# Named PSUM banks in two feed-forward layers, a later Silu and modulation stream, sums on VectorE, and a third ordinary pair in the last two

## The chip, the cores and the metric

The kernel runs as one program on one core of a Trainium2 chip. The core has five engines that work side by side, each through its own queue in order: TensorE (PE in the rows; its weight loads, PEld, overlap it), VectorE (DVE), ScalarE (ACT), GpSimd (POOL) and SyncE (SP), which issues the transfers. They wait for one another by semaphores. TensorE writes its results into PSUM, which has eight banks; one 128x512 tile of float32 fills a bank. The metric is the time of one execution on the device in microseconds (us).

## What is computed

A float32 tensor x of 512 tokens by 1024 channels goes through eight residual stages: an attention mixer and a feed-forward layer with modulation, twice, then a state-space mixer, a feed-forward layer, a convolution module and a feed-forward layer, and a last norm. The stages of the change are the four feed-forward layers. In the first block they read

```python
cond = jax.nn.silu(c)
mod = cond @ ada_w[l] + ada_b[l]
sh1, sc1, g1, sh2, sc2, g2 = [m[:, None, :] for m in jnp.split(mod, 6, axis=-1)]
...
h = _rms_norm(x, norm_ffn[l]) * (1.0 + sc2) + sh2
x = x + g2 * _swiglu(h, ffn_gate[l], ffn_up[l], ffn_down[l])
```

and in the second `h = h + swiglu_ffn(rmsnorm(h, ffn_norm[i]), w_gate, w_up, w_down)`, where swiglu is `(silu(h @ wg) * (h @ wu)) @ wd` with a hidden width of 2816, 22 chunks of 128.

## The kernel before

**Layout and products.** x is kept transposed, as eight chunks of 128 channels by 512 tokens (`xT`, `X[c]`). Every float32 product is three matmuls: each operand is split into a rounded part `hi` and a rest `lo`, and `mm3` (and the same lines in `lin`) issues hi·hi (L305), lo·hi (L306) and hi·lo (L307) into one accumulator. The split of a weight is one cast on ScalarE (L297) and one subtraction on VectorE (L298), each 1024 wide; weights come by a load on SP (L291, or L708 in `seven`), through three buffers.

**Stages.** They run in the order mix0, ffn0, mix1, ffn1, ssm, ffn2, conv, ffn3, final. Each has its own PSUM pool. Within a stage the code is written as items and woven streams, and a scheduler then sets each engine's order at build time.

**The norm ahead of a stage.** ffn0 and ffn1 use the class `Split`, which works on halves of 256 tokens: `stats` puts the sums of squares into a PSUM tile `ss` (L462) and takes the reciprocal root on VectorE (it begins with `rm`, L345); `spread` broadcasts it into a PSUM tile `rb` (L471); `build` makes, for each chunk, z = x·gain·rb on VectorE (L481), hi on ScalarE (L491, or L487 and L488), and lo on VectorE for even chunks (L492) and on GpSimd for odd ones (L489). `Split.lin` interleaves this with the first two hidden chunks: all matmuls of the first half, 256 wide, then those of the second. A half of the two pairs of accumulators `pg` and `pu` is 96 matmuls, six for a chunk and pair. ffn2 and ffn3 use the class `Norm`: the matmuls run on data without the scale, `rb` (L374) is copied to `R` on ScalarE (L427), and the scale is multiplied in behind the products (L794, L796).

**The modulation.** `cond` loads c into `cb` (L625) and applies Silu (L626). `Mod.stream` takes a column pair at a time: load `araw` (L641), multiply by `cb` and sum on VectorE (L651). In ffn0 a stream of 28 such pairs, 56 products, is woven into the layer, behind `nm.mark`, the last z.

**Pairs in a feed-forward layer.** For each of the 22 hidden chunks there is one pair of gate and up products. An ordinary pair has 48 matmuls of 128x512. From number FIRST_S[n] on, the pairs use `seven`, which replaces eight half products by seven, 84 matmuls of 128x256, and for that needs sums of quarters of the normed data. `sums` makes them with `crossed`, for k = 0 to 3 (chunks k and k + 4): two subtractions on GpSimd (L687, L688), two on VectorE (L689, L690), a cast `xh` on ScalarE (L692) and the rest `xl` on VectorE for even k and on GpSimd for odd k (L693). In ffn2 and ffn3 the z for it comes from ScalarE (L761). FIRST_S was (22, 3, 2, 2): ffn0 has ordinary pairs only, ffn1 three, ffn2 and ffn3 two.

**Banks.** The six accumulators, one tile for sums and one for broadcasts were given to the pool by counts (`"mm": 6, "st": 1, "tr": 1`), and the pool set the banks. In both ffn0 and ffn1 the first `pg` had bank 0, the first `pu` bank 5, and the next ones 4, 3, 2 and 1; `ss` had 6 and `rb` 7 in the layer. The tiles of the mixer ahead, the `rb` of the first half among them, have their banks from that mixer's pool: the bank of `rb` was 0 ahead of ffn0 and 5 ahead of ffn1.

## Time and profile before

| | us |
|---|---|
| median of three runs | 2677.18 |
| the runs | 2670.21, 2677.18, 2677.36 |
| profiled execution | 2673.64 |
| its span, first to last instruction | 2671.9 |
| time around the span | 1.7 |
| mean granted TensorE clock | 0.974 |

Where the profile speaks of idle time before an instruction, the bracket names what released it. ffn0 runs from about 369 to 739 us in it, ffn1 from 945 to 1310, ffn2 from 1725 to 2065 and ffn3 from 2310 to 2645.

### The profile page before, as it was taken

To read this page: it belongs to the slowest core of one execution; us is meant where nothing else is said; L and a number is where in the kernel's file an instruction comes from. 1 tells how busy PE (TensorE), PEld (TensorE's weight loads), DVE (VectorE), ACT (ScalarE), POOL (GpSimd) and SP (SyncE) were. 2 spreads that over 40 slices of the span, in tenths; PEclk is the share of its full clock that TensorE was granted. 3 is DMA by queue.
4 is the path that set the end of the run, shared out by engine and by line. 5 is a ranking of instruction groups with operands and counts; after the bars stand their busy time and mean duration, and the time that the engine had idled before them with its cause. 6 is when DMAs were issued, how large, how long until landed. Compare 5 with 4: busy or idle time off the path is not lost.

```text
span 2671.9 us, 39622 instructions
## 1 busy us (share of the span) xinstructions
PE 2529.7 (95%) x15167; PEld 2231.6 (84%) x15167; DVE 1943.4 (73%) x3437; ACT 1261.9 (47%) x2324; POOL 549.1 (21%) x394
## 2 busy tenths in 40 slices
PE   5887989999999989999999999999999998899998
PEld 3666888888888889999788888789999788799997
DVE  8898756555556686677678887678677797678776
ACT  4456642222357554544455444455445555545443
POOL 3344220000112250000100000131012683321102
PEclk9889999999999989999999999999999998999999
DMA  7711025555421113333322121223333110133332
GB/s 262 238 56 40 32 87 205 174 167 199 146 81 41 40 64 95 101 99 104 110 73 72 52 87 59 81 81 108 104 103 109 66 63 17 64 112 101 102 98 87
DMA packets 84734, 265.77 MB, mean 99 GB/s; under 512 B 9280, under 2 KB 11712, under 8 KB 84544
## 3 DMA queue, kind: packets, MB, share of 16 engines
q1 hardware_dynamic: 84544, 263.24, 30.4%
q8 instruction: 119, 1.95, 0.3%
q14 instruction: 71, 0.58, 0.1%
HBM read 261.10 MB, written 2.10 MB: 99 GB/s over the span
## 4 chain that ended last, share of the span: by engine, by line
PE 72%; DVE 14%; ACT 4%; issue 3%; POOL 3%; DMA 3%; SPq 0%; DVEq 0%; POOLq 0%; ACTq 0%
PE pj L305 10%; PE pj L306 9%; PE pj L307 9%; PE pg L305 6%; PE pg L307 6%; PE pg L306 5%; PE pu L305 4%; PE pu L306 4%; PE pu L307 4%; DVE lo L298 2%; DMA raw<-w_gu 1%; POOL yp L1609 1%; DMA araw<-ada 1%; PE pj L1412 1%; PE pj L1413 1%
## 5 line engine op out<-in xcount | busy, mean ns | idle before, releaser
L297 ACT CAST hi<-raw 128x1024 fp32r<-128x1024 f32 (+5 forms) x445 | 393.7, 893 | 691.7 <-PE pj L306 260.5
L298 DVE TENSOR_TENSOR lo<-raw,hi 128x1024 fp32r<-128x1024 f32 (+5 forms) x435 | 461.6, 1064 | 175.2 <-ACT hi L297 172.1
L305 PE MATMUL pj<-d,hi 128*128 128x512 f32 (+1 forms) x940 | 354.3, 385 | 3.3 <-DVE xT L679 1.7
L306 PE MATMUL pj<-d,hi 128*128 128x512 f32 (+1 forms) x940 | 354.6, 380 | 0.0
L307 PE MATMUL pj<-d,lo 128*128 128x512 f32 (+1 forms) x940 | 351.5, 380 | 0.0
L741 POOL TENSOR_TENSOR bu<-bu 128x256 f32<-128x256 f32 x59 | 110.0, 1864 | 770.6 <-ACT bu L737 754.5
L305 PE MATMUL pu<-hi 128*128 128x256 f32 (+1 forms) x736 | 230.2, 314 | 3.2 <-DVE z L481 3.2
L307 PE MATMUL pu<-hi,lo 128*128 128x256 f32 (+1 forms) x736 | 231.1, 314 | 0.2 <-DVE lo L298 0.2
L306 PE MATMUL pu<-lo,hi 128*128 128x256 f32 (+1 forms) x736 | 229.9, 313 | 0.0
L305 PE MATMUL pj<-hi 128*128 128x512 f32 (+2 forms) x520 | 207.7, 403 | 3.9 <-ACT qk L901 1.2
L306 PE MATMUL pj<-lo,hi 128*128 128x512 f32 (+2 forms) x520 | 207.1, 398 | 3.6 <-DVE lo L492 2.4
L305 PEld LDWEIGHTS pj<-d,hi 128*128 128x128 f32 x940 | 177.7, 190 | 38.0 <-DVE xT L679 2.3
L306 PEld LDWEIGHTS pj<-d,hi 128*128 128x128 f32 x940 | 178.3, 190 | 33.2 <-issue 1.0
L307 PEld LDWEIGHTS pj<-d,lo 128*128 128x128 f32 x940 | 177.9, 189 | 33.3 <-issue 0.5
L307 PE MATMUL pj<-hi,lo 128*128 128x512 f32 (+2 forms) x520 | 204.8, 395 | 0.3 <-DVE lo L298 0.3
L305 PE MATMUL pg<-xh,hi 128*128 128x256 f32 x708 | 199.3, 282 | 0.8 <-ACT ua L734 0.7
L305 PE MATMUL pg<-hi 128*128 128x256 f32 (+1 forms) x572 | 192.6, 337 | 6.9 <-DVE z L481 4.5
L307 PE MATMUL pg<-xh,lo 128*128 128x256 f32 x708 | 198.0, 280 | 0.0
L306 PE MATMUL pg<-xl,hi 128*128 128x256 f32 x708 | 198.0, 280 | 0.0
L307 PE MATMUL pg<-hi,lo 128*128 128x256 f32 (+1 forms) x572 | 192.4, 336 | 4.8 <-DVE lo L298 4.8
L306 PE MATMUL pg<-lo,hi 128*128 128x256 f32 (+1 forms) x572 | 191.6, 335 | 0.6 <-DVE lo L492 0.6
L297 ACT CAST hi<-ws 128x1024 fp32r<-128x1024 f32 x118 | 123.5, 1049 | 116.7 <-DVE ws L711 48.5
(485 smaller groups left out, 6390.7 us busy)
## 6 DMA issues: line engine op xcount, KB each, us to landing
raw<-w_gu SPq DMA_DIRECT2D x176, 512.0 KB, 3.8
araw<-ada SPq DMA_DIRECT2D x96, 512.0 KB, 5.9
raw<-w_dn SPq DMA_DIRECT2D x48, 384.0 KB, 3.2
raw<-w_dn SPq DMA_DIRECT2D x48, 320.0 KB, 3.0
raw<-w_p SPq DMA_DIRECT2D x24, 512.0 KB, 3.6
raw<-w_out SPq DMA_DIRECT2D x32, 256.0 KB, 2.8
raw<-w_xs SPq DMA_DIRECT2D x16, 512.0 KB, 3.4
raw<-w_z SPq DMA_DIRECT2D x16, 512.0 KB, 3.4
```

What stands on the lines that cost most here:

```text
L297: S.copy(hi, raw)
L298: (eng or V).tensor_tensor(lo, raw, hi.bitcast(F32), op=OP.subtract)
L305: E.matmul(ps, lh, rh, start=start, stop=False, **k)
L306: E.matmul(ps, lh, rl, start=False, stop=False, **k)
L307: E.matmul(ps, ll, rh, start=False, stop=stop, **k)
L741: G.tensor_tensor(bu[:, :hv], bu[:, :hv], bu[:, hv:], op=OP.add)
L1412: E.matmul(o, xh[:, ts], wh[:, k], start=st_, stop=False, skip_group_check=True)
L1413: E.matmul(o, xh[:, ts], wl[:, k], start=False, stop=False, skip_group_check=True)
L1609: G.tensor_tensor(yp[:, sft:], yp[:, sft:], pr[:, sft:], op=OP.add)
```

## The change

It has four parts. In ffn0 and ffn1 the PSUM banks are named; with the lists below, the first `pg` of ffn0 has bank 7 and the first `pu` 4, those of ffn1 7 and 6; `ss` and `rb` have 1 and 6, and 4 and 5. In ffn0 the Silu of `cb` becomes a step that is emitted after four others, and the modulation stream comes behind `nm.lmark`, the last lo of the norm, and has weight 30. In ffn1 the sums of `crossed` are all on VectorE, two k behind the first item and two behind the second. FIRST_S becomes (22, 3, 3, 3): in ffn2 and ffn3 the third pair is an ordinary one. Lines from 245 on stand some ten lines lower in the code of the change.

```diff
-FIRST_S = (22, 3, 2, 2)
+FIRST_S = (22, 3, 3, 3)
...
-    "ffn0": ({"araw": 6, "cb": 2, "d": 16, "z": 3, "su": 2, "sq": 2}, {"mm": 6, "st": 1, "tr": 1}),
-    "ffn1": ({"d": 12, "z": 8, "sq": 2, "ws": 3, "xh": 4, "xl": 4, "ua": 2, "bu": 2}, {"mm": 6, "st": 1, "tr": 1}),
+    "ffn0": ({"araw": 6, "cb": 2, "d": 16, "z": 3, "su": 2, "sq": 2},
+             {"mm": (7, 4, 2, 3, 0, 5), "st": (1,), "tr": (6,)}),
+    "ffn1": ({"d": 12, "z": 8, "sq": 2, "ws": 3, "xh": 4, "xl": 4, "ua": 2, "bu": 2},
+             {"mm": (7, 6, 0, 1, 2, 3), "st": (4,), "tr": (5,)}),
...
+            if k == "ps" and isinstance(PHASES[name][1]["mm" if name != "start" else "pi"], tuple):
+                turn.clear()
+                for b in range(8):
+                    p.tile([128, T], F32, tag=f"b{b}", name=f"b{b}", bufs=1)
...
+        if isinstance(bufs[tag], tuple):
+            i = turn[tag] = turn.get(tag, -1) + 1
+            return p.tile(shape, dt, tag=f"b{bufs[tag][i % len(bufs[tag])]}", name=name, bufs=1)
...
-                    V.scalar_tensor_tensor(lo, z, sh, hi_.bitcast(F32), op0=OP.add, op1=OP.subtract)
+                    self.lmark = V.scalar_tensor_tensor(lo, z, sh, hi_.bitcast(F32), op0=OP.add, op1=OP.subtract)
...
-        S.activation(cbx[0], cbx[0], AF.Silu)
+        return lambda: S.activation(cbx[0], cbx[0], AF.Silu)
...
-    def crossed(k, z1, z2, pool_lo):
+    def crossed(z1, z2, eng, lo_eng):
...
-        G.tensor_tensor(q[0], z1[:, :hv], z1[:, hv:], op=OP.subtract)
-        G.tensor_tensor(q[2], z2[:, hv:], z1[:, hv:], op=OP.subtract)
+        eng.tensor_tensor(q[0], z1[:, :hv], z1[:, hv:], op=OP.subtract)
+        eng.tensor_tensor(q[2], z2[:, hv:], z1[:, hv:], op=OP.subtract)
...
-        (G if pool_lo else V).tensor_tensor(lo, t, hi.bitcast(F32), op=OP.subtract)
+        lo_eng.tensor_tensor(lo, t, hi.bitcast(F32), op=OP.subtract)
...
-                x4.append(crossed(k, *z, k % 2))
+                x4.append(crossed(*z, V if direct else G, G if k % 2 and not direct else V))
...
-                    sums(range(4) if direct else range(2 * js[0], 2 * js[0] + 2))
+                    sums(range(len(x4), len(x4) + 2))
...
-                cond()
-                _weave((f, 345), (behind(lambda: nm.mark, chain(md0.stream(range(20, 24)), md1.stream(range(24)))), 28))
+                silu = cond()
+
+                def later():
+                    for _ in range(4):
+                        yield 0.5
+                    silu()
+                    yield 0.0
+
+                _weave((f, 345), (chain(later(), behind(lambda: nm.lmark, chain(md0.stream(range(20, 24)),
+                                                                               md1.stream(range(24))))), 30))
```

The scheduler makes of this new orders on the engines at the starts of the four layers, and in ffn0 for the modulation through the whole layer; mix0, mix1, the body of ssm and conv keep theirs. In the rows that follow, the numbers are those of the buffers, and lines of the changed kernel are its own.

VectorE in ffn0, from the last lo of the second half (`lo_3493`) to the first weight split of the third and fourth pair of operands (L298, `lo_3814` before and `lo_3809` after); first before, then with the change.

```order
L492 SCALAR_TENSOR_TENSOR lo_3493<-z_3680,mod0_95,hi_3492 128x256
L651 ISA araw_3808,mod0_95<-araw_3808,cb_3513,vec_71 128x1024
L651 ISA mod0_95 128x1
L651 ISA araw_3880,mod0_95<-araw_3880,cb_3513,vec_71 128x1024
L651 ISA mod0_95 128x1
L651 ISA araw_3883,mod0_95<-araw_3883,cb_3513,vec_71 128x1024
L651 ISA mod0_95 128x1
L298 TENSOR_TENSOR lo_3814<-raw_3811,hi_3813 128x1024
```

```order
L502 SCALAR_TENSOR_TENSOR lo_3493<-z_3687,mod0_95,hi_3492 128x256
L661 ISA araw_3876,mod0_95<-araw_3876,cb_3521,vec_71 128x1024
L661 ISA mod0_95 128x1
L661 ISA araw_3879,mod0_95<-araw_3879,cb_3521,vec_71 128x1024
L661 ISA mod0_95 128x1
L308 TENSOR_TENSOR lo_3809<-raw_3806,hi_3808 128x1024
```

Before, three products of the modulation stood ahead of that lo and three between it and the split; with the change two stand between them and none ahead. On ScalarE the Silu of `cb` has the same place in both orders, behind the first half's build and ahead of the second's, and on SP the load of `cb` stands behind two loads of `w_gu` in both, with six loads of `araw` behind it before and two with the change.

VectorE in ffn1, up to the weight split for the first ordinary-width matmuls (`lo_8978` before, `lo_8974` after).

```order
L492 SCALAR_TENSOR_TENSOR lo_8624<-z_8666,mod1_100,hi_8623 128x256
L689 SCALAR_TENSOR_TENSOR ws_8923<-z_8664,ws_8923 128x256
L690 SCALAR_TENSOR_TENSOR ws_8923<-ws_8923,z_8664 128x256
L689 SCALAR_TENSOR_TENSOR ws_8932<-z_8665,ws_8932 128x256
L690 SCALAR_TENSOR_TENSOR ws_8932<-ws_8932,z_8665 128x256
L689 SCALAR_TENSOR_TENSOR ws_8943<-z_8666,ws_8943 128x256
L690 SCALAR_TENSOR_TENSOR ws_8943<-ws_8943,z_8666 128x256
L693 TENSOR_TENSOR xl_8929<-ws_8923,xh_8928 128x1024
L693 TENSOR_TENSOR xl_8949<-ws_8943,xh_8948 128x1024
L298 TENSOR_TENSOR lo_8978<-raw_8975,hi_8977 128x1024
```

```order
L699 SCALAR_TENSOR_TENSOR ws_9035<-z_8682,ws_9035 128x256
L700 SCALAR_TENSOR_TENSOR ws_8939<-ws_8939,z_8680 128x256
L700 SCALAR_TENSOR_TENSOR ws_8948<-ws_8948,z_8681 128x256
L700 SCALAR_TENSOR_TENSOR ws_9035<-ws_9035,z_8682 128x256
L703 TENSOR_TENSOR xl_8945<-ws_8939,xh_8944 128x1024
L703 TENSOR_TENSOR xl_8954<-ws_8948,xh_8953 128x1024
L697 TENSOR_TENSOR ws_9044<-z_8679 128x256
L698 TENSOR_TENSOR ws_9044<-z_8683,z_8679 128x256
L703 TENSOR_TENSOR xl_9041<-ws_9035,xh_9040 128x1024
L699 SCALAR_TENSOR_TENSOR ws_9044<-z_8683,ws_9044 128x256
L308 TENSOR_TENSOR lo_8974<-raw_8971,hi_8973 128x1024
```

Before, six sums of three k and two `xl` stood ahead of the split on VectorE, and the subtractions L687 and L688 and the `xl` of odd k on GpSimd. With the change 15 operations of sums and three `xl` (L703) stand there, of which the last eleven rows are shown, and GpSimd has none.

TensorE in ffn2 behind the broadcast `rb`; `pg_16453` and `pu_16454` are the second ordinary pair before and `pg_16565` is the first `seven`; with the change `pu_16470` is of the second pair and `pg_16567` and `pu_16568` are the third. First before, at `rb`,

```order
L374 MATMUL rb_16424<-cst_73,rstd_16405 128x128 x4
L307 MATMUL pu_16454<-hi_16242,lo_16450 128x512
L305 MATMUL pg_16453<-hi_16269,hi_16443 128x512
L306 MATMUL pg_16453<-lo_16270,hi_16443 128x512
L307 MATMUL pg_16453<-hi_16269,lo_16444 128x512
L305 MATMUL pu_16454<-hi_16269,hi_16449 128x512
```

then before, on TensorE a few rows on, at the end of the second pair,

```order
L306 MATMUL pg_16453<-lo_16297,hi_16443 128x512
L307 MATMUL pg_16453<-hi_16296,lo_16444 128x512
L305 MATMUL pu_16454<-hi_16296,hi_16449 128x512
L306 MATMUL pu_16454<-lo_16297,hi_16449 128x512
L307 MATMUL pu_16454<-hi_16296,lo_16450 128x512
L305 MATMUL pg_16565<-hi_16108,hi_16545 128x256
```

and last with the change, from `rb` on.

```order
L384 MATMUL rb_16440<-cst_73,rstd_16421 128x128 x4
L315 MATMUL pu_16470<-hi_16312,hi_16465 128x512
L316 MATMUL pu_16470<-lo_16313,hi_16465 128x512
L317 MATMUL pu_16470<-hi_16312,lo_16466 128x512
L315 MATMUL pg_16567<-hi_16124,hi_16557 128x512
L316 MATMUL pg_16567<-lo_16125,hi_16557 128x512
L317 MATMUL pg_16567<-hi_16124,lo_16558 128x512
L315 MATMUL pu_16568<-hi_16124,hi_16563 128x512
```

Before, 13 matmuls of 512 stood between `rb` and the first `seven`; with the change `rb` is ten matmuls later, and 51 of 512 stand behind it. ffn3 has the same change. In all, 72 matmuls fewer are issued.

## Rows read from the trace of the kernel before

**Rows 1.** The page: busy time of each engine in us, share of the span and instructions, and the share of each engine in the chain of work that ended last.

```profile
PE 2529.7 (95%) x15167; PEld 2231.6 (84%) x15167; DVE 1943.4 (73%) x3437; ACT 1261.9 (47%) x2324; POOL 549.1 (21%) x394
...
PE 72%; DVE 14%; ACT 4%; issue 3%; POOL 3%; DMA 3%; SPq 0%; DVEq 0%; POOLq 0%; ACTq 0%
```

**Rows 2.** Windows, a stretch in the middle of ffn0: from and to, length, busy time (with the count of instructions) of PE, PEld, DVE, ACT and POOL, granted TensorE clock, mean share of the DMA engines, GB/s.

```profile
420.00:520.00 100.00, 100.00 (x441) 82.43 (x440) 53.55 (x75) 23.96 (x28) 0.00 (x0) 1.00 0.52 173
```

**Rows 3.** Timeline of PE at the start of ffn0: start in us, duration, engine, line, operation, out<-in, shape, count, and in brackets the idle time before it and what ended it.

```profile
367.00 0.53 PE L471 MATMUL rb<-cst,rstdh 128*128 128x128 f32 x2
...
373.41 0.36 PE L305 MATMUL pg<-hi 128*128 128x256 f32 x1 [4.47 <-DVE z L481]
...
374.24 0.42 PE L305 MATMUL pg<-hi 128*128 128x256 f32 x1
...
398.65 0.40 PE L305 MATMUL pg<-hi 128*128 128x512 f32 x1
...
401.87 0.80 PE L307 MATMUL pg<-hi,lo 128*128 128x512 f32 x1 [2.59 <-DVE lo L298]
...
404.95 0.40 PE L305 MATMUL pg<-hi 128*128 128x512 f32 x1
```

**Rows 4.** Timelines of PE, ACT and POOL from the end of the ssm stage to the first seven pair of ffn2, with the same columns.

```profile
1721.72 0.39 PE L305 MATMUL pu<-hi 128*128 128x512 f32 x1
...
1727.61 0.39 PE L307 MATMUL pu<-hi,lo 128*128 128x512 f32 x1
...
1737.62 0.60 PE L374 MATMUL rb<-cst,rstd 128*128 128x128 f32 x4
...
1741.03 0.28 PE L305 MATMUL pg<-hi 128*128 128x256 f32 x1
...
1743.78 0.28 PE L307 MATMUL pu<-hi,lo 128*128 128x256 f32 x1
1746.72 0.58 PE L305 MATMUL pu<-xh,hi 128*128 128x256 f32 x1 [2.66 <-ACT hi L297]
...
1749.46 0.58 PE L307 MATMUL pu<-xh,lo 128*128 128x256 f32 x1 [1.51 <-DVE lo L298]
...
1753.73 0.28 PE L307 MATMUL pu<-xh,lo 128*128 128x256 f32 x1
...
1745.62 1.04 ACT L297 CAST hi<-ws 128x1024 fp32r<-128x1024 f32 x1
...
1748.22 5.23 POOL L693 TENSOR_TENSOR xl<-ws,xh 128x1024 fp32r<-128x1024 f32 x1 [5.65 <-ACT xh L692]
```

**Rows 5.** Timeline of PE at the start of ffn1.

```profile
951.66 0.55 PE L305 MATMUL pu<-hi 128*128 128x256 f32 x1 [3.17 <-DVE z L481]
...
957.56 0.62 PE L462 MATMUL ss<-ones,acc 128*128 128x1 f32 x4
...
978.18 0.40 PE L305 MATMUL pg<-hi 128*128 128x512 f32 x1
...
980.57 0.50 PE L307 MATMUL pg<-hi,lo 128*128 128x512 f32 x1 [1.76 <-DVE lo L298]
...
984.92 0.49 PE L305 MATMUL pg<-hi 128*128 128x512 f32 x1
```

**Rows 6.** Timeline of PE at the first seven pair of ffn3.

```profile
2329.91 0.28 PE L307 MATMUL pu<-hi,lo 128*128 128x256 f32 x1
2332.85 0.39 PE L305 MATMUL pu<-xh,hi 128*128 128x256 f32 x1 [2.65 <-ACT hi L297]
...
2335.58 0.58 PE L307 MATMUL pu<-xh,lo 128*128 128x256 f32 x1 [1.92 <-DVE lo L298]
...
2340.22 0.28 PE L306 MATMUL pg<-xl,hi 128*128 128x256 f32 x1
```

**Rows 7.** Timelines of DVE and ACT at the start of ffn0.

```profile
376.68 0.47 DVE L492 SCALAR_TENSOR_TENSOR lo<-z,mod,hi 128x256 fp32r<-128x256 f32 x1
...
384.50 1.06 ACT L626 ACTIVATE cb<-cb 128x1024 f32<-128x1024 f32 x1 [8.96 <-DMA cb<-c]
...
398.13 1.28 DVE L651 CUSTOM_DVE_ANT_0 araw<-araw,cb,vec 128x1024 f32<-128x1024 f32 x1 [1.52 <-DMA araw<-ada]
...
400.60 1.22 DVE L298 TENSOR_TENSOR lo<-raw,hi 128x1024 fp32r<-128x1024 f32 x1
```

**Rows 8.** Timeline of DVE at the start of ffn1.

```profile
954.95 0.95 DVE L492 SCALAR_TENSOR_TENSOR lo<-z,mod,hi 128x256 fp32r<-128x256 f32 x1
...
958.23 0.16 DVE L345 TENSOR_SCALAR rm<-ss 128x2 f32<-128x2 f32 x1 [2.32 <-PE ss L462]
...
965.69 2.69 DVE L492 SCALAR_TENSOR_TENSOR lo<-z,mod,hi 128x256 fp32r<-128x256 f32 x4
969.01 0.94 DVE L689 SCALAR_TENSOR_TENSOR ws<-z,ws 128x256 f32<-128x256 f32 x1 [0.63 <-POOL ws L687]
...
974.28 4.57 DVE L693 TENSOR_TENSOR xl<-ws,xh 128x1024 fp32r<-128x1024 f32 x2
978.77 1.75 DVE L298 TENSOR_TENSOR lo<-raw,hi 128x1024 fp32r<-128x1024 f32 x1
...
981.04 0.41 DVE L689 SCALAR_TENSOR_TENSOR ws<-z,ws 128x256 f32<-128x256 f32 x1
```

**Rows 9.** Waits of DVE from 365 to 740 us, which is ffn0: what waited and for whom, us in total, times, longest.

```profile
DVE araw L651 <- DMA araw<-ada: 85.1, 28, 6.7
```

More of the change, by code (lines that the diff above doesn't have):

```diff
@@ L231, in _program @@
     cur = {"sb": None, "ps": None}
+    turn = {}
     def phase(name, kinds=("sb", "ps")):
@@ L491, in build @@
                     S.activation(hi_, z, AF.Identity, bias=sh)
-                    V.scalar_tensor_tensor(lo, z, sh, hi_.bitcast(F32), op0=OP.add, op1=OP.subtract)
+                    self.lmark = V.scalar_tensor_tensor(lo, z, sh, hi_.bitcast(F32), op0=OP.add, op1=OP.subtract)
                 else:
                     S.copy(hi_, z)
-                    V.tensor_tensor(lo, z, hi_.bitcast(F32), op=OP.subtract)
+                    self.lmark = V.tensor_tensor(lo, z, hi_.bitcast(F32), op=OP.subtract)
         def lin(self, sets, at=(5, 10)):
@@ L974, in mix0 @@
         phase("start", ("ps",))
-        cond()
+        cond()()
         consts()
@@ L1798, in _program @@
         if stages[0] in STAGES[:4]:
-            cond()
+            cond()()
             mods()
@@ L1821, in _program @@
             if n == 0:
-                cond()
-                _weave((f, 345), (behind(lambda: nm.mark, chain(md0.stream(range(20, 24)), md1.stream(range(24)))), 28))
+                silu = cond()
[6 more added lines that the diff above has]
+                                                                               md1.stream(range(24))))), 30))
             else:
```

## The prediction

> **What bounds the kernel now.** I read the busy shares first: TensorE (PE) is busy 95% of the span, and the chain that ended last lies to 72% on PE and to 14% on VectorE (DVE) [rows 1]. So time is to be had only where PE stands still or runs at the lower clock, and I looked for those places in PE's timeline. The body of the first feed-forward layer shows none: in 420 to 520 us PE is busy for 100.00 of 100 us at a granted clock of 1.00 [rows 2]. The gaps lie at the starts of the four feed-forward layers, where the norm's result has to be built, and these are the places that the change touches.
>
> In ffn0 PE sees the broadcast `rb` at 367.00 and issues the first gate matmul at 373.41, after 4.47 us idle that ended with a z (L481) on DVE [rows 3]. A matmul on one half cannot need all z of that half; it waits because its accumulator lies in the bank that holds `rb`, which every z reads. Then its 256-wide matmuls take 0.21 instead of 0.12 us for a while (from 374.24 on, the granted clock at the 1.2 GHz level after the idle time). At 401.87 a second gap ends: 2.59 us for one `lo` (L298) on DVE, and the seven 512-wide matmuls from there to 404.95 take 3.08 us, where seven at the usual 0.2265 us take 1.59 (26 starts between 1721.72 and 1727.61, 5.89 us) [rows 3, 4]. ffn1 has the same pair of gaps: 3.17 us at 951.66, here on `pu`, and 1.76 us at 980.57 [rows 5]. ffn2 and ffn3 have theirs at the first `seven` pair: 2.66 and 1.51 us, and 2.65 and 1.92 us [rows 4, 6].
>
> **ffn0: banks, and the modulation behind the last lo.** Six new banks keep the first gate and up accumulators away from that of `rb`, so the 4.47 us goes. It is not won in full, since the data come late too: the `lo` of chunk 6 ends on DVE at 376.68 + 0.47 = 377.15, behind two weight splits, and the change moves neither [rows 7]. At that time PE will have done six chunks, 36 of the half's 96 matmuls. The other 60 take 60 x 0.12 = 7.2 us, with the four `ss` half a microsecond more: about 385. The second half cannot start then: ScalarE's Silu of `cb` waits 8.96 us for its DMA and runs 384.50 to 385.56, and the second half's `hi` are queued behind it [rows 7]. The change makes this Silu a step of its own that is issued later; yet on ScalarE it stands at the same place in the order as before, and its DMA at the same place on SP, behind two loads of w_gu. So the second half starts near 386.0 and, paced by its `hi` and `lo`, ends about 0.7 us before 398.65. What does move is on DVE: of the six modulation products (L651, some 1.3 us each) that stood ahead of the split L298 at 400.60, one of them waiting 1.52 us for its own DMA, two remain, so the split comes before PE asks for it [rows 7]. That removes the 2.59 us and the lower clock behind it (3.08 - 1.59 = 1.5). Sum: 0.7 + 2.6 + 1.5 = **4.8**. Lower bound 0.7 (the split still late), upper bound 6 (data a little earlier as well). I take 4.5.
>
> **ffn1: banks, and the sums on DVE.** The banks remove the 3.17 us and the lower clock up to 957.56 [rows 5]; what comes next is again chunk 6's `lo`, which ends at 954.95 + 0.95 = 955.90 [rows 8]. Its matmuls wait for it, but the `ss` that starts the second half's rsqrt no longer ends after 957.56: DVE's `rm`, at 958.23 after a wait of 2.32 us for PE, can start right behind the `lo` [rows 8], which brings all of the second half 2.3 us forward. For the sums, DVE had six operations at about 0.9 us beside GpSimd (POOL), two L693 in 4.57 us, and then the split L298 in 1.75; alone, a sum takes 0.41 (the row of 981.04) and a 1024-wide split 1.22 [rows 7, 8]. Now 15 sums and three L693 stand ahead of that split: back to back 15 x 0.34 + 3 x 1.14 = 8.5 us (both durations less the 0.07 by which neighbours overlap). They start where the last `lo` ends, 968.38 - 2.3 = 966.1 [rows 8], so the split runs 974.6 to 975.8. PE wants it 2.3 us before 978.18 + 0.46, at 976.3 [rows 5]: just in time. So 2.3 + 1.76 and, if no gap is left, the lower clock of 981.9 to 984.9 (about 1.5): 5.6. Half a microsecond of lateness would bring a good part of the last term back; I take **4.5**, bounds 1.8 and 6.
>
> **ffn2 and ffn3: one more ordinary pair.** Between the last ordinary-data matmul of the first `seven` (1743.78, next due 1743.90) and the return to the full pace (1753.73) PE does 21 matmuls of 256 in 9.83 us; at 0.12 they take 2.5, so 7.3 us are lost in ffn2; in ffn3, from 2330.03 to 2340.22, 22 matmuls, 10.19 - 2.63 = 7.6 us [rows 4, 6]. All of it hangs on one chain that starts at `rb`: its hi is done 9.0 us after 1737.62 (ScalarE, 1745.62 + 1.04), its lo 11.8 us after, and POOL's xl 15.8 us after (1748.22 + 5.23) [rows 4]. Before, PE puts 13 ordinary matmuls and 24 of the `seven` behind `rb` and then needs them: 6.2 us. With the third ordinary pair there stand 51 and 24: 51 x 0.2265 + 2.9 + 0.4 = 14.8 us. `rb` itself moves ten matmuls later, but the distance is what counts. A second weight split now ahead of that chain on DVE adds some 1.2 us: hi at 10.2, lo at 13, both early; xl at 17 and wanted about a dozen matmuls after the first, 16.3. I leave 0.5 us of stall. The price is 48 x 0.2265 = 10.9 us in place of 84 x 0.12 = 10.05, so +0.8 per layer (with the rows unrounded). Net: 7.3 - 0.8 - 0.5 = **6.0** and 7.6 - 0.8 - 0.5 = **6.3**; at worst only the wait for hi goes (2.66 - 0.8 = 1.8 each), at best 6.5 and 6.8.
>
> The rows say that a 512-wide matmul takes 0.2265 and a 256-wide one 0.12 us, so a column costs 6% more in the small one. The Trainium skill, Perfetto Trace Analysis, section Optimizing Tensor Performance, says that larger matmuls are more efficient than smaller ones. The trace agrees; if columns alone counted, 84 small ones would take 9.5 us, the pair would cost 1.4 instead of 0.8, and the sum would be 1.1 us smaller.
>
> **Sum.** 4.5 + 4.5 + 6.0 + 6.3 = 21.3. The profiled execution took 2673.64 us (span 2671.9, 1.7 around it): 2652.3. The three runs before have a median of 2677.18, 3.5 above it, which gives 2655.9. I take **2654**.
>
> **Rivals.** (1) The stall of ffn2 and ffn3 moves with the `seven`. Then the pairs cost 1.6 and bring nothing, and only the starts gain: 2673.6 to 2677.2 less 9.0 plus 1.6, 2666 to 2670. For it: POOL's xl takes 5.2 us beside DVE's long splits. Against: everything that is late there hangs on `rb`, and PE's distance to it more than doubles. (2) The starts of ffn0 and ffn1 gain almost nothing: the Silu isn't moved on ScalarE, chunk 6's `lo` isn't either, and the split in ffn1 arrives late once more behind 18 operations. Then 12.3 + 1 remain: about 2662. The Trainium skill, SBUF — State Buffer, section Who interferes with whom, has it that a VectorE instruction with two SBUF inputs and a GpSimd instruction that reads SBUF lock each other out. By that rule the sums run at 0.41 only if POOL has nothing to do there; the order leaves it one L489 in that stretch, and the trace agrees (0.94 beside POOL, 0.41 alone). (3) Slower: the modulation stream in ffn0. It is still 56 L651, and DVE already waits 85.1 us, 28 times and up to 6.7, for their DMAs [rows 9]. They are now spread among the weight splits from the second pair on; a wait in front of a split holds that split, and PE behind it. If 1.5 us per pair reached PE in 20 pairs, that is 30 us: 2684. It makes the kernel slower from 1.1 us per pair on. Against: the same waits cost PE nothing in 420 to 520.
>
> **How the numbers follow.** The forecast has 0.66, rival 1 0.12, rival 2 0.16, rival 3 0.06. A measurement of this kernel tells 0.3% (8 us) from no change: under 2669 is faster. The forecast and rival 2 lie below it, rival 1 half on either side, and of rival 3 two thirds lie above 2685: faster 0.66 + 0.16 + 0.06 = 0.88, same 0.06 + 0.02 = 0.08, slower 0.04. For the range, the four upper bounds together (25.3) from the profiled run give 2648, and with the lowest run before 2645; at the other end rival 1 in its better half: 2646 to 2667.
>
> **What would show it.** In the profile after: in ffn0 the first `pg` within 2 us of `rb` and no wait for `lo` L298; in ffn1 no wait of `pu` for z, `rm` near 956 on the old scale, and no GpSimd sums; in ffn2 and ffn3 no PE wait for hi or lo at the first `seven`, and 72 fewer matmuls. It is wrong if PE waits in the bodies of ffn0 or ffn1, or if the waits at the first `seven` come back under the names of ScalarE or POOL.

## The result and the profile after

| | before | changed | ratio, 95% interval |
|---|---|---|---|
| first series, median of 5 and 5 runs | 2674.05 us | 2659.49 us (2652.77 to 2662.43) | 0.9933 [0.9918, 0.9948] |
| second series, the changed kernel once more, 11 and 6 runs | 2675.04 us | 2655.88 us (2649.92 to 2658.43) | 0.9923 [0.9909, 0.9937] |
| profiled execution, first series | 2673.64 us | 2652.77 us | |

The medians fall by 15 and 19 us (by the intervals of the ratio 14 to 24), to 2659.5 and 2655.9 us, where 2654 had been forecast. The ratio is not the quotient of the two medians. The profiled execution is the fastest of its series. Its page, busy times and the chain that ended last, to be held against [rows 1]:

```profile
PE 2526.1 (95%) x15095; PEld 2223.6 (84%) x15095; DVE 1938.1 (73%) x3431; ACT 1255.6 (47%) x2312; POOL 522.9 (20%) x382
...
PE 70%; DVE 15%; issue 4%; DMA 4%; ACT 4%; POOL 3%; SPq 0%; POOLq 0%; DVEq 0%; ACTq 0%
```

The span is 20.9 us shorter. PE has the 72 matmuls less and is busy only 3.6 us less, so 17.3 us are idle time that went. So the places where PE waited come next.

**ffn0.** Timelines of PE and ACT at its start, of SP's queue, and SP's waits from 355 to 378 us (what waited and for whom, us in total, times, longest), in the changed kernel (against [rows 3, 7]):

```profile
365.78 0.63 PE L481 MATMUL rb<-cst,rstdh 128*128 128x128 f32 x2
...
367.66 0.28 PE L315 MATMUL pg<-hi 128*128 128x256 f32 x1
368.56 0.39 PE L316 MATMUL pg<-lo,hi 128*128 128x256 f32 x1 [0.62 <-DVE lo L502]
...
369.99 0.39 PE L316 MATMUL pg<-lo,hi 128*128 128x256 f32 x1 [0.43 <-POOL lo L499]
...
376.05 0.39 PE L316 MATMUL pg<-lo,hi 128*128 128x256 f32 x1 [1.07 <-DVE lo L502]
...
384.45 0.38 PE L315 MATMUL pg<-hi 128*128 128x256 f32 x1 [0.87 <-ACT hi L501]
...
397.20 0.39 PE L317 MATMUL pg<-hi,lo 128*128 128x512 f32 x1
```

```profile
382.94 1.06 ACT L636 ACTIVATE cb<-cb 128x1024 f32<-128x1024 f32 x1 [8.54 <-DMA cb<-c]
```

```profile
356.68 19.31 SPq L301 DMA_DIRECT2D raw<-w_gu  x3
376.04 0.43 SPq L635 DMA_DIRECT2D cb<-c  x1
```

```profile
SPq L301 <- DVE lo L308: 23.2, 3, 16.9
```

The 4.47 us in front of the first `pg` are gone (it comes 1.88 us behind `rb`), and so is the bracket at the 512-wide L317. What is left are 0.62 and 0.43 us for the `lo` of the first two chunks, 1.07 us for chunk 6's `lo` and 0.87 us for `hi` behind the Silu. SP's rows show why the Silu is late: of the three weight loads that stand in one row there, one waits 16.9 us for a weight split (L308), the last two are issued at 373.99 and 375.66, and only then comes the load of `cb`.

**ffn1.** Timeline of PE (against [rows 5]): the 3.17 us for a z are gone, and at the first 512-wide matmuls at most 0.31 is left of the 1.76, but in between stand two waits of over a microsecond, and 14 matmuls 0.21 us apart (granted clock 0.50 from 947.0 to 949.9).

```profile
946.55 0.58 PE L316 MATMUL pg<-lo,hi 128*128 128x256 f32 x1 [1.54 <-DVE lo L502]
946.93 0.41 PE L317 MATMUL pg<-hi,lo 128*128 128x256 f32 x1
...
949.50 0.41 PE L317 MATMUL pg<-hi,lo 128*128 128x256 f32 x1
...
952.15 0.41 PE L481 MATMUL rb<-cst,rstdh 128*128 128x128 f32 x2 [1.10 <-DVE rstdh L372]
...
1292.32 0.47 PE L315 MATMUL pj<-hi 128*128 128x512 f32 x1 [1.35 <-DVE xT L685]
```

**ffn2 and ffn3.** PE from `rb` to the first `seven` pair, whose first matmuls carry no bracket now (against [rows 4, 6]), then a wait in ffn2's body and one at its end, and the DVE row that the first goes back to:

```profile
1728.53 0.60 PE L384 MATMUL rb<-cst,rstd 128*128 128x128 f32 x4
...
1740.55 0.28 PE L315 MATMUL pg<-hi 128*128 128x256 f32 x1
1740.67 0.28 PE L316 MATMUL pg<-lo,hi 128*128 128x256 f32 x1
```

```profile
2323.48 0.28 PE L315 MATMUL pg<-hi 128*128 128x256 f32 x1
2323.59 0.28 PE L316 MATMUL pg<-lo,hi 128*128 128x256 f32 x1
```

```profile
1830.40 0.39 PE L317 MATMUL pu<-hi,lo 128*128 128x256 f32 x1 [0.77 <-DVE lo L308]
...
2054.20 0.39 PE L315 MATMUL pj<-d,hi 128*128 128x256 f32 x1 [2.43 <-DVE xT L689]
```

```profile
1827.91 0.69 DVE L720 TENSOR_TENSOR ws<-raw 128x512 f32<-128x512 f32 x1 [2.10 <-DMA raw<-w_gu]
```

**By stage.** Two tables hold all profiles of this study together. The first gives the length of a stage in us, from the first `ss` matmul of its norm to that of the next stage; mix0 and conv, which nothing below touches, are left out.

| kernel | ffn0 | mix1 | ffn1 | ffn2 | ffn3 |
|---|---|---|---|---|---|
| before | 378.1 | 201.4 | 367.9 | 343.3 | 338.2 |
| changed | 371.7 | 196.9 | 367.5 | 340.1 | 331.9 |
| changed_again | 373.7 | 201.3 | 368.1 | 338.8 | 331.8 |
| third_pair_alone | 378.6 | 197.3 | 372.8 | 337.4 | 332.1 |
| starts_alone | 373.8 | 201.3 | 368.2 | 343.8 | 339.0 |
| sums_on_gpsimd | 371.5 | 197.0 | 370.2 | 338.3 | 330.7 |
| old_stream | 375.5 | 201.4 | 366.8 | 337.2 | 332.6 |
| split_behind_lo | 370.8 | 202.9 | 369.4 | 337.7 | 331.6 |
| silu_own_queue | 369.9 | 201.3 | 367.3 | 337.2 | 333.9 |
| both_starts | 369.4 | 202.9 | 368.0 | 337.2 | 332.1 |
| adds_behind_rsqrt | 373.5 | 196.9 | 367.8 | 337.6 | 331.1 |
| adds_and_silu | 371.4 | 201.4 | 367.0 | 336.1 | 334.1 |
| all_three | 369.4 | 196.8 | 367.9 | 337.7 | 331.5 |

The second counts the gate and up matmuls in ffn0 and ffn1 from the layer's first `rb` on, from 0, and gives when certain of them start, in us behind that `rb`: number 192 is the first 512-wide one, 232 comes some 9 us later at full pace, 500 is well into the body. "rb 2" is the second half's broadcast in ffn1.

| kernel | ffn0: 192 | 232 | 500 | ffn1: rb 2 | 192 | 232 | 500 |
|---|---|---|---|---|---|---|---|
| before | 31.65 | 45.00 | 149.76 | 16.78 | 32.88 | 45.32 | 111.25 |
| changed | 30.95 | 40.05 | 144.81 | 16.33 | 32.40 | 42.15 | 108.21 |
| changed_again | 32.97 | 42.06 | 146.82 | 16.24 | 33.60 | 42.32 | 108.37 |
| third_pair_alone | 31.60 | 46.66 | 151.42 | 16.59 | 32.70 | 43.54 | 113.12 |
| starts_alone | 33.00 | 42.09 | 146.85 | 16.46 | 32.53 | 42.29 | 108.35 |
| sums_on_gpsimd | 30.59 | 39.68 | 144.44 | 16.32 | 32.40 | 43.28 | 109.54 |
| old_stream | 31.21 | 43.57 | 148.33 | 16.26 | 33.74 | 42.46 | 108.51 |
| split_behind_lo | 28.55 | 37.65 | 142.41 | 16.31 | 33.88 | 42.59 | 108.64 |
| silu_own_queue | 29.15 | 38.24 | 143.00 | 16.26 | 33.78 | 42.50 | 108.55 |
| both_starts | 28.58 | 37.67 | 142.44 | 16.31 | 34.30 | 43.02 | 109.07 |
| adds_behind_rsqrt | 31.25 | 40.34 | 145.10 | 13.08 | 30.25 | 42.87 | 108.93 |
| adds_and_silu | 29.13 | 38.23 | 142.99 | 13.05 | 30.23 | 42.79 | 108.86 |
| all_three | 28.56 | 37.65 | 142.41 | 12.76 | 29.97 | 43.67 | 109.74 |

Comparing one program with itself (changed and changed_again) shows what such a reading is worth: 2.0 us in ffn0, 4.4 in mix1, 0.6 in ffn1, 1.3 in ffn2, 0.1 in ffn3. Kernels that share a stage's code differ by more: ffn1 takes 367.9 us in the kernel before and 372.8 in third_pair_alone, which edits ffn2 and ffn3 alone (in one place of it PE waits 1.90 us for a `hi`, where the kernel before does not), and ffn3 takes 330.7 to 334.1 with the third pair. Part of the difference is the clock ahead of `rb`: from the first `ss` to the first `rb` of ffn0 and ffn1 the same matmuls take 4.5 us in one profile and 6.1 in another. So a stage by itself is known to some 2 us in ffn0 and 5 in ffn1; the second table, which starts at `rb`, is the sharper one. Of the 20.9 us between the two profiled executions, the 4.5 in mix1 are therefore not the change's.

### The profile page after: what moved, and what is told of

It reads as the page before. It is cut to its first block, busy times and chain, and to the rows that moved or that the text cites. A ratio compares the mean times of both kernels' runs of the same rounds, so it can differ in the third digit from the quotient of the medians.

```text
span 2651.0 us, 39434 instructions
## 1 busy us (share of the span) xinstructions
PE 2526.1 (95%) x15095; PEld 2223.6 (84%) x15095; DVE 1938.1 (73%) x3431; ACT 1255.6 (47%) x2312; POOL 522.9 (20%) x382
## 4 chain that ended last, share of the span: by engine, by line
PE 70%; DVE 15%; issue 4%; DMA 4%; ACT 4%; POOL 3%; SPq 0%; POOLq 0%; DVEq 0%; ACTq 0%
PE pj L315 9%; PE pj L316 9%; PE pj L317 9%; PE pg L315 5%; PE pg L317 5%; PE pg L316 5%; PE pu L317 4%; PE pu L315 4%; PE pu L316 4%; DVE lo L308 3%; DMA raw<-w_gu 2%; POOL yp L1619 1%; PE pj L1422 1%; PE pj L1423 1%; PE pj L1424 1%
## 5 line engine op out<-in xcount | busy, mean ns | idle before, releaser
L308 DVE TENSOR_TENSOR lo<-raw,hi 128x1024 fp32r<-128x1024 f32 (+5 forms) x435 | 465.8, 1074 | 166.8 <-ACT hi L307 161.8
L317 PE MATMUL pj<-d,lo 128*128 128x512 f32 (+1 forms) x940 | 351.2, 379 | 0.0
L751 POOL TENSOR_TENSOR bu<-bu 128x256 f32<-128x256 f32 x57 | 96.8, 1697 | 783.4 <-ACT bu L747 718.9
L317 PE MATMUL pu<-hi,lo 128*128 128x256 f32 (+1 forms) x736 | 232.0, 315 | 0.9 <-DVE lo L308 0.9
L317 PE MATMUL pj<-hi,lo 128*128 128x512 f32 (+2 forms) x520 | 205.8, 397 | 0.3 <-DVE lo L308 0.3
L317 PEld LDWEIGHTS pj<-d,lo 128*128 128x128 f32 x940 | 177.5, 189 | 33.4 <-issue 0.5
L317 PE MATMUL pg<-hi,lo 128*128 128x256 f32 (+1 forms) x580 | 194.7, 336 | 1.9 <-DVE lo L308 1.9
L315 PE MATMUL pg<-xh,hi 128*128 128x256 f32 x684 | 191.7, 280 | 0.5 <-ACT ua L744 0.2
L316 PE MATMUL pg<-xl,hi 128*128 128x256 f32 x684 | 190.5, 279 | 0.0
L317 PE MATMUL pg<-xh,lo 128*128 128x256 f32 x684 | 190.5, 278 | 0.0
```

The lines of the kernel that those rows point to most:

```text
L308: (eng or V).tensor_tensor(lo, raw, hi.bitcast(F32), op=OP.subtract)
L315: E.matmul(ps, lh, rh, start=start, stop=False, **k)
L316: E.matmul(ps, lh, rl, start=False, stop=False, **k)
L317: E.matmul(ps, ll, rh, start=False, stop=stop, **k)
L751: G.tensor_tensor(bu[:, :hv], bu[:, :hv], bu[:, hv:], op=OP.add)
```

## The experiments

My theory was that of the sum: the starts of ffn0 and ffn1 and the third pair in ffn2 and ffn3 each win their part. The rivals gave the whole gain to the pairs, or held that the waits only move. The first four kernels take the change apart, in one series with 20 runs of the kernel before (median 2676.46 us).

**third_pair_alone**: the kernel before with one edit.

```diff
-FIRST_S = (22, 3, 2, 2)
+FIRST_S = (22, 3, 3, 3)
```

> The kernel before with only the third ordinary pair in ffn2 and ffn3. Theory A (the waits at the first seven go, each layer on its own): no PE wait for hi or lo at the first seven; the start of ffn2 6.0 us shorter and that of ffn3 6.3; part of ffn2's comes back later in the layer in waits of PE for L298, as in the changed kernel (some 2 to 3 us), so 9 to 12 us faster than before. Rival (the gain of these two layers in the profile was luck of that run, the changed kernel's profile being its fastest): the starts differ by under 2 us each, within 4 us of before.

Measured: 2661.53 us, 0.9949 [0.9933, 0.9965], some 14 us less: theory A, with a little more than its 9 to 12. The stage table has it in ffn2 (-5.8) and ffn3 (-6.1). In ffn0 the old stall stands, with 3.03 us:

```profile
402.62 0.80 PE L307 MATMUL pg<-hi,lo 128*128 128x512 f32 x1 [3.03 <-DVE lo L298]
```

**starts_alone**: the changed kernel without the pairs.

```diff
-FIRST_S = (22, 3, 3, 3)
+FIRST_S = (22, 3, 2, 2)
```

> The changed kernel with the third ordinary pair taken back: banks, later stream and sums on VectorE alone. Theory A: ffn0 5 us shorter from its rb to the end of the stage, ffn1 1 to 3 us, ffn2 and ffn3 as before: 5 to 8 us faster than before. The theory of the prediction, by which ffn1's start is worth as much as ffn0's: 9 us. Rival (the parts only work together): no more than 2 us.

Measured: 2668.32 us, 0.9972 [0.9959, 0.9984], some 8 us less: theory A at its upper end. At matmul 500 ffn0 and ffn1 are each 2.9 us ahead of the kernel before. Both parts work, and 14 and 8 make up the gain of the whole (15 to 19) within the intervals. ffn2's first `seven` has its waits again:

```profile
1744.60 0.39 PE L315 MATMUL pu<-xh,hi 128*128 128x256 f32 x1 [2.67 <-ACT hi L307]
...
1747.33 0.58 PE L317 MATMUL pu<-xh,lo 128*128 128x256 f32 x1 [1.99 <-DVE lo L308]
```

**sums_on_gpsimd**: the changed kernel with ffn1's sums on GpSimd, and all of them behind the first item, as before.

```diff
-                x4.append(crossed(*z, V if direct else G, G if k % 2 and not direct else V))
+                x4.append(crossed(*z, G, G if k % 2 else V))
...
-                    sums(range(len(x4), len(x4) + 2))
+                    sums(range(4) if direct else range(len(x4), len(x4) + 2))
```

> The changed kernel with the sums of ffn1 as before: subtractions and odd xl on GpSimd, all four k behind the first item. Theory A (VectorE is slowed beside GpSimd, and PE then waits for the split): PE waits about 1.8 us for L308 at the end of ffn1's first pairs and runs at the lower clock for some 3 us behind it, 3 to 4 us slower than the changed kernel. Rival (the banks alone moved the half, the sums are off the path): no wait, within 1 us of the changed kernel.

Measured: 2655.34 us, 0.9931 [0.9910, 0.9952]: in the time not to be told from the changed kernel. The trace does show a price. The stall of [rows 5] is back with the same 1.76 us, and matmul 232 of ffn1 starts 1.1 us later than in the changed kernel, too little for the runs to show. So the wait is that of theory A, and its price a third of the 3 to 4 us expected. At matmul 500 ffn1 is 1.7 us ahead of the kernel before with the banks alone, and 3.0 with the sums on VectorE as well:

```profile
970.63 0.50 PE L317 MATMUL pg<-hi,lo 128*128 128x512 f32 x1 [1.76 <-DVE lo L308]
```

**old_stream**: the changed kernel with the Silu at once, and the modulation stream behind the last z with the old weight.

```diff
-                silu = cond()
-
-                def later():
-                    for _ in range(4):
-                        yield 0.5
-                    silu()
-                    yield 0.0
-
-                _weave((f, 345), (chain(later(), behind(lambda: nm.lmark, chain(md0.stream(range(20, 24)),
-                                                                               md1.stream(range(24))))), 30))
+                cond()()
+                _weave((f, 345), (behind(lambda: nm.mark, chain(md0.stream(range(20, 24)), md1.stream(range(24)))), 28))
```

> The changed kernel with the Silu at once and the modulation stream of ffn0 behind the last z with weight 28, as before. Theory A (the products L661 ahead of the weight split make PE wait): the wait of 2.6 us for L308 is back in ffn0 and the lower clock behind it, 4 us slower than the changed kernel. Rival (with the banks PE's half ends earlier or later so that the split is in time anyway): no wait, within 1 us.

Measured: 2660.70 us, 0.9941 [0.9920, 0.9961]. The first weight split of the 512-wide matmuls is late again; matmul 500 of ffn0 starts at 148.33 against 144.81 and 146.82. So the later Silu and stream are worth 1.5 to 3.5 us where 4 had been expected, and the 1.4 us that ffn0 keeps (149.76 before) are those of the banks:

```profile
399.24 0.50 PE L317 MATMUL pg<-hi,lo 128*128 128x512 f32 x1 [2.97 <-DVE lo L308]
```

What stayed open was ffn1, where of 4.5 us forecast some 3 had come at matmul 500, and the two waits left in ffn0. The next four run in one series with 11 runs of the kernel before (2675.04 us).

**changed_again**: no edit.

> The changed kernel once more, unaltered, beside the others. What two of its profiles differ by in stages that nobody touched is the uncertainty of the readings by stage. Theory A (the 4.5 us between 196.9 and 201.3 us in mix1, and the 2 to 3 us given back in ffn2, vary from run to run): ffn0 371 to 372.5, ffn3 331 to 333, while mix1 may show either 197 or 201.3 and ffn2 337 to 341. Theory B (they belong to the code): mix1 197 and ffn2 340 again, within 0.5. Time by both: 2653 to 2663.

Measured: 2655.88 us, 0.9923 [0.9909, 0.9937]; mix1 takes 201.3 us this time.

**split_behind_lo**

```diff
-                    with tc.issue_after(nm.mark.ins) if direct and j == 1 else nullcontext():
+                    with tc.issue_after(nm.lmark.ins) if direct and j == 1 else nullcontext():
```

> The changed kernel with one word changed: in ffn0 and ffn1 the weight splits of the second half pair come behind the last lo of the norm's first half, not behind its last z. Theory A (ffn1 got less than forecast because TensorE waits for chunk 6's lo, which stands behind two 1024-wide splits on VectorE): in ffn1 the 1.54 us wait for that lo (946.55 in the changed kernel) and the lower clock behind it (15 matmuls at 0.21 instead of 0.12, about 1.4 us) go, in ffn0 the 1.07 us wait; by the end of the half 2 to 3 us are won in ffn1 and up to 1 in ffn0, if the second half's rsqrt does not take it back. Theory B (the second half in ffn1 is bound by the rsqrt beside GpSimd's adds, 946.42 to 952.0): the wait goes and the wait for rb (1.10 us) grows by as much; nothing within 0.3 us at the first 512-wide matmul. Time: A 2655 to 2657, B 2659.

Measured: 2655.75 us, 0.9920 [0.9901, 0.9939]. In ffn1 theory B holds: the 1.54 us for the `lo` are gone, and the wait for the second `rb` is 4.39 us, where changed_again has 2.58. On VectorE the two weight splits stand ahead of the root in both orders, so it begins only half a microsecond earlier (10.1 us behind the first `rb` against 10.6); what they cost there was not tried.

```profile
959.30 0.40 PE L481 MATMUL rb<-cst,rstdh 128*128 128x128 f32 x2 [4.39 <-DVE rstdh L372]
```

In ffn0 more was won than expected, and for another reason. Moving the splits also moved their loads on SP; the load of `cb` is issued at 359.12 instead of 376.04, and the Silu waits for nothing:

```profile
358.75 0.33 SPq L301 DMA_DIRECT2D raw<-w_gu  x1
359.12 0.43 SPq L635 DMA_DIRECT2D cb<-c  x1
```

**silu_own_queue**

```diff
-    def cond():
+    def cond(q=nc.sync):
...
-        nc.sync.dma_start(cbx[0], a["c"].to_broadcast([128, 1024]))
+        q.dma_start(cbx[0], a["c"].to_broadcast([128, 1024]))
...
-                silu = cond()
+                silu = cond(nc.scalar)
```

> The changed kernel with the load of c for the Silu in ffn0 issued by ScalarE's own queue instead of SP's, where it stands behind two loads of weights. Theory A (the second half of ffn0 is held by this load: the Silu waits 8.54 us for it, to 382.94, with the half's hi queued behind it): the Silu waits under 3 us, the second half's hi come before TensorE wants them, and the 0.87 us wait of TensorE for hi at 384.45 goes; ffn0 gains 0.9 to 1.5 us. Theory B (the load is late for lack of bandwidth beside the weights, not for its place in SP's queue): the wait stays over 6 us and nothing is won. Time: A 2658, B 2659.5; the runs alone cannot tell these, the wait in the trace can.

Measured: 2652.01 us, 0.9920 [0.9906, 0.9934]. Theory A for the wait: the Silu's falls from 8.54 to 2.23 us, the wait for `hi` at the second half is gone, and matmul 500 of ffn0 starts 1.8 us earlier than in the changed kernel (3.8 earlier than in changed_again). Theory B has a part in it all the same: behind the first `rb` the load is issued 3.4 us earlier (6.9 against 10.3 us), and the other 3.0 us are a shorter way from issue to landing, 3.9 us instead of 6.9. Why the way is shorter isn't shown. First the Silu, then the load's row (KB, us from issue to landing) here and in the changed kernel:

```profile
376.38 1.06 ACT L636 ACTIVATE cb<-cb 128x1024 f32<-128x1024 f32 x1 [2.23 <-DMA cb<-c]
```

```profile
cb<-c ACTq DMA_DIRECT2D x1, 512.0 KB, 3.9
cb<-c SPq DMA_DIRECT2D x1, 512.0 KB, 6.9
```

**both_starts**: the two edits together.

> Both edits together: the splits behind the last lo, and the load of c on ScalarE's queue. If each removes its wait, ffn0 has neither the 1.07 us wait for lo nor the 0.87 us wait for hi, and ffn1 not the 1.54 us: 3 to 5 us less than the changed kernel, 2654.5 to 2656.5. If the waits only move (to rb in ffn1, to the weight splits at the second half pair in both), 2658 to 2660.

Measured: 2653.84 us, 0.9915 [0.9899, 0.9931]. ffn0 is as in split_behind_lo (142.44); ffn1 is held by its second `rb` as there. The gains don't add, since both removed the same wait of the Silu.

That left the reciprocal root in ffn1, to be tried with 11 runs of the kernel before (2672.84 us).

**adds_behind_rsqrt**: the changed kernel with the eight adds moved into `build`.

```diff
                     self.gmark = G.tensor_tensor(lo, z, hi_.bitcast(F32), op=OP.subtract)
+                    with tc.issue_after(self.gmark.ins):
+                        for k in (c - 1, c) if hf and self.keep else ():
+                            p, (u, w) = HALVES[0], self.h[k]
+                            G.tensor_tensor(self.keep[k][:, p], u[:, p].bitcast(F32), w[:, p].bitcast(F32), op=OP.add)
...
-                        for z, (hi, lo) in zip(nm.keep, h):
-                            o = HALVES[0]
-                            G.tensor_tensor(z[:, o], hi[:, o].bitcast(F32), lo[:, o].bitcast(F32), op=OP.add)
```

> The changed kernel with one thing moved: in ffn1, GpSimd's eight adds that restore the first half (hi + lo, 6.7 us back to back) stand between its lo of the second half, two behind each, so that none runs beside VectorE's reciprocal root. Theory A (ffn1's second half is bound by that root, whose 14 small operations take 5.6 us beside these adds and 2.3 us in ffn0, where GpSimd is idle): the root takes under 3 us, the second rb comes 13 to 14 us behind the first instead of 16.2 to 16.8, and the first 512-wide matmul about 31 us behind it instead of 32.4 to 33.6. Theory B (the root is slow for another reason, and rb stays 16 us behind): no change by more than 0.3 us. The price: VectorE's z and lo of the second half now run beside the adds, and a new wait of TensorE for them may take back up to 2 us. Time: A 2653 to 2656, B 2656 to 2659.

Measured: 2652.68 us, 0.9927 [0.9907, 0.9947]. Theory A holds for the root. DVE and POOL in the changed kernel, first and last operations of the root in ffn1:

```profile
946.42 0.15 DVE L355 TENSOR_SCALAR rm<-ss 128x2 f32<-128x2 f32 x1
946.60 0.51 DVE L360 TENSOR_SCALAR ri<-rm 128x2 int32<-128x2 int32 x1
...
947.14 0.65 DVE L361 TENSOR_SCALAR rj<-ri 128x2 int32<-128x2 int32 x1
947.83 1.33 DVE L368 SCALAR_TENSOR_TENSOR rt<-rj,rh 128x1 f32<-128x1 f32 x2
949.20 0.65 DVE L372 SCALAR_TENSOR_TENSOR rstdh<-rt,rj 128x2 f32<-128x2 f32 x1
...
951.84 0.16 DVE L372 SCALAR_TENSOR_TENSOR rstdh<-rt,rstdh 128x2 f32<-128x2 f32 x1
```

```profile
944.52 6.69 POOL L787 TENSOR_TENSOR z<-hi,lo 128x256 f32<-128x256 f32 x8
```

in the kernel before, where the root had begun later (958.23, [rows 8]) and the adds ended in its middle,

```profile
961.86 0.16 DVE L362 SCALAR_TENSOR_TENSOR rstdh<-rt,rstdh 128x2 f32<-128x2 f32 x1
```

```profile
953.91 6.73 POOL L777 TENSOR_TENSOR z<-hi,lo 128x256 f32<-128x256 f32 x8
```

and in adds_behind_rsqrt, where GpSimd is idle meanwhile:

```profile
945.60 0.15 DVE L355 TENSOR_SCALAR rm<-ss 128x2 f32<-128x2 f32 x1
945.78 0.17 DVE L360 TENSOR_SCALAR ri<-rm 128x2 int32<-128x2 int32 x1
...
945.99 0.17 DVE L361 TENSOR_SCALAR rj<-ri 128x2 int32<-128x2 int32 x1
946.19 0.35 DVE L368 SCALAR_TENSOR_TENSOR rt<-rj,rh 128x1 f32<-128x1 f32 x2
...
947.74 0.16 DVE L372 SCALAR_TENSOR_TENSOR rstdh<-rt,rstdh 128x2 f32<-128x2 f32 x1
```

The root, 13 operations, falls from 5.58 (946.42 to 952.00) to 2.30 us; before it had taken 3.79 (958.23 to 962.02). The single records show how it is held. In the changed kernel the last seven adds end at 947.08, 947.77, 948.46, 949.14, 949.82, 950.51 and 951.21, and seven operations of the root end 0.02 to 0.03 us behind them, one behind each add; the rest of the root runs at its short durations. changed_again shows the same seven pairs, split_behind_lo eight.

With the adds moved, the second `rb` comes 13.08 us behind the first, and the first 512-wide matmul 2.2 us earlier than in the changed kernel. But nothing is left of it 40 matmuls later (42.87 against 42.15): the sums on VectorE now run beside the adds, 0.96 us each instead of 0.41 (the first seven of them), and the split behind them comes too late:

```profile
965.75 0.50 PE L315 MATMUL pg<-hi 128*128 128x512 f32 x1 [0.97 <-ACT hi L307]
...
968.40 0.50 PE L317 MATMUL pg<-hi,lo 128*128 128x512 f32 x1 [1.91 <-DVE lo L308]
```

**adds_and_silu**: this and the edit of silu_own_queue.

> The same move of the adds, and the load of c on ScalarE's queue as in silu_own_queue. If the two gains are each their own: ffn0 near 370 us from its first sum of squares to that of mix1, as in silu_own_queue (369.9), and ffn1's second rb 13 to 14 us behind the first. Time 2649 to 2653 if they add, 2652 to 2656 if the gain of ffn1 is given back at its end.

Measured: 2648.98 us, 0.9914 [0.9894, 0.9933]. ffn0's gain is there (142.99 at matmul 500), ffn1's is given back as above.

**all_three**: with the edit of split_behind_lo as well.

> The adds moved, the load of c on ScalarE's queue, and the weight splits behind the last lo of the first half. With the root no longer slow, the wait for chunk 6's lo (1.54 us) should be won when it goes, where it only lengthened the wait for rb in split_behind_lo (2.58 to 4.39 us): first 512-wide matmul of ffn1 about 30 us behind the first rb. If the splits, which then stand in front of the root, hold it by their 2.9 us: no better than adds_and_silu. Time 2647 to 2651, or 2649 to 2653.

Measured: 2651.38 us, 0.9915 [0.9895, 0.9935]. The first 512-wide matmul of ffn1 is the earliest of all (29.97), and matmul 500 is later than in the changed kernel (109.74 against 108.21). The whole start of that layer looks held by VectorE's sums and splits, wherever PE's wait stands; a kernel with fewer of them was not tried.

Of all kernels adds_and_silu has the lowest median, but its interval overlaps with both of the changed kernel's. What the traces carry is 1.8 to 3.8 us, from the load of `cb` in ffn0.

## Why the prediction was right, and where not

The forecast case came about: every stall named at the four starts went, and the time lies in the range. The sum was 21.3 us; by the tables the parts are these.

- **ffn0: forecast 4.5, measured 4.95 and 2.94** (matmul 500, changed and changed_again against before). The steps hold: the first `pg` comes within 2 us of `rb`; chunk 6's `lo` ends 10.2 us behind `rb`, as before, and PE waits for it; the second half waits for the Silu; the split at the first 512-wide matmul is early. The two profiles differ by how late the load of `cb` lands (Silu waiting 8.54 and 9.34 us): PE then waits 0.87 and 1.66 us for `hi`, and behind the longer wait it has a granted clock of 0.66 for 5 us instead of 1.00. old_stream brings the wait for the split back and nothing else.
- **ffn1: forecast 4.5, measured 3.0 and 2.9 at matmul 500, and 0.4 or less over the stage.** The step that failed is "which brings all of the second half 2.3 us forward". It had the root start 2.3 us earlier, which it does (10.6 us behind the first `rb` instead of 12.9), and took its duration, 3.79 us in the kernel before, for given; but the root then runs almost wholly beside GpSimd's adds and takes 5.58 us, and the second `rb` comes 0.5 us earlier, no more. The first 512-wide matmul starts at 32.40 and 33.60 us, before at 32.88: the term of 2.3 measured 0.5 and -0.7. adds_behind_rsqrt shows the cause, split_behind_lo that PE's wait for the `lo` is not one. The other term of the sum, the split and the clock behind it, was worth 2.2 and measured 2.7 and 3.7 (from matmul 192 to 232, 12.44 against 9.75 and 8.72 us; the old code takes 10.84 in third_pair_alone). That the 15 sums fit ahead of the split held too: it starts at 967.87 and PE hardly waits.
- **ffn1 behind its start.** Of what was won, some 0.8 us is given back at the hand-over to ssm: `pj` waits 1.35 us for `xT` (1292.32), and a wait behind it is 0.4 us shorter. A wait of 1.31 to 1.35 us stands there in nearly every kernel with the named banks (0.60 in both_starts), and in neither of the two without; but one of these, third_pair_alone, waits 0.89 us for a `lo` there and loses as much, so it isn't shown that the banks cost anything. In the changed kernel another 1.2 us are the clock ahead of the first `rb` (6.14 us from `ss` against 4.93), in changed_again PE waits some 0.3 us at a time for splits late in the layer. Against third_pair_alone, which has the old ffn1 too, the changed kernel's is 5.3 us shorter: by the stage this layer's gain stays open, by its start the failed step is shown. The sum looked at the start alone.
- **ffn2: forecast 6.0, measured 3.1 and 4.4** by the stage table. The start is right to the row: no wait is left at the first `seven`, not even the half microsecond for `xl`. But 1.5 to 2.5 us more of waits than before then stand in the body and at the layer's end, for splits behind weights that land late (L720 waits 2.10 us for its DMA) and for `xT` (2.43 and 2.03 us, before 1.33). In the other profiles with the third pair ffn2 takes 336.1 to 338.3 us, 5 to 7 less than before, so this part varies between executions and belongs to no edit.
- **ffn3: forecast 6.3, measured 6.3 and 6.4**, and 4.1 to 7.5 in the other kernels with the third pair.
- **The rivals.** The first, that the stall moves with the `seven`, fell with the rows above. The second was half right, for ffn1 alone and for a reason that it did not name. The third fell: from 400 to 740 us PE waits nowhere in ffn0, though the stream's products stand among the splits.
- **The time.** By the changed kernel's two profiles the parts are 4.9 + 0.4 + 3.1 + 6.3 = 14.7 and 2.9 - 0.2 + 4.4 + 6.4 = 13.5, against 14.6 and 19.2 between the medians. 2654 was too low by 2 to 5.5 us. By the profiles that lies in ffn1 and in ffn2's body; the profile of the kernel before is a single one, with a shorter ffn1 than third_pair_alone, so it is not settled which of the two counts for more.

The Trainium skill, SBUF — State Buffer, section Who interferes with whom, was drawn on in the prediction for the sums alone, and I did not apply it to the root. It says that a VectorE instruction with two SBUF inputs contends with a GpSimd instruction that reads SBUF. The root's rows agree: two L368, which have two, take 1.33 us together beside the adds and 0.35 without, an L372 0.65 and 0.16. For an instruction with one SBUF input it expects contention only in certain modes, which it says `tensor_scalar` can enter; here `ri` and `rj`, `tensor_scalar` with one, took 0.51 and 0.65 us instead of 0.17. Which mode they ran in no row shows.

## What to carry to other kernels

When a step is brought forward, look at what the other engines do in its new place, and price it with a duration from such a place: the root cost 2.3 us alone and 5.6 us beside eight adds. If removing a wait of the bounding engine only lengthens the next one, as twice in ffn1, count the work of the engine that feeds it over the whole stretch; here it seems to be that total which has to shrink. A load behind loads that wait on the same queue is as late as they are; issuing it on another queue, or ahead of them, took the Silu's wait from 8.54 to 2.23 and to 0.01 us here. And before a difference of a few us in one stage is put down to an edit, compare two profiles of the same code there.

## What was not expected of the hardware

The stage mix1, which no edit touches, takes 196.8 to 197.3 us in five of thirteen profiles and 201.3 to 202.9 in eight, the same program among both. The difference is a stretch at the lower clock behind waits of PE of well under a microsecond each. The stretch that makes most of it is the same 28 matmuls, from a `pT` to a `pj`; its window (from and to, length, busy times, granted clock, DMA share, GB/s) in the kernel before, the changed kernel and changed_again:

```profile
845.14:851.72 6.58, 6.58 (x31) 6.18 (x29) 3.20 (x15) 3.12 (x13) 2.19 (x3) 0.50 0.00 0
```

```profile
838.99:842.49 3.50, 3.50 (x31) 3.32 (x29) 2.83 (x15) 2.92 (x13) 2.17 (x3) 1.00 0.00 0
```

```profile
841.11:847.61 6.50, 6.50 (x29) 6.17 (x29) 2.96 (x15) 2.85 (x12) 2.04 (x2) 0.51 0.01 3
```

PE is busy throughout in all three, for 6.58, 3.50 and 6.50 us at granted clocks of 0.50, 1.00 and 0.51. In the 4 us ahead of it PE has the same four waits in each, of 0.33 to 0.34, 0.45 to 0.46, 0.27 to 0.28 and 0.21 to 0.22 us. Why the clock falls in some executions and not in others stays open. A single pair of profiles would have given 4.5 us of it to the change.
